# Gated convolution's input: five block groups and four plain tiles on operands without the row factor, in place of four groups and eight tiles

## The chip, the cores and the metric

The kernel runs on one core of a Trainium2 chip. The metric is the device time of one execution in microseconds (us). The kernel before was run three times, and the median counts. One further execution was recorded by the hardware profiler, and every duration in this document that is read from a trace of the kernel before comes from it.

## What is computed

The reference is a four-layer decoder trunk in float32 for one sequence of 512 positions and 1024 features: attention, a gated MLP, a gated short convolution, a gated MLP. Each layer normalises its input, computes a branch and adds it to the residual. Only the third layer's input is touched here:

```python
def rms_norm(x, g):
    xf = x.astype(jnp.float32)
    y = xf * lax.rsqrt(jnp.mean(xf * xf, axis=-1, keepdims=True) + EPS)
    return (y * g.astype(jnp.float32)).astype(x.dtype)

def causal_dwconv(x, w):
    k = w.shape[0]
    s = x.shape[1]
    xp = jnp.pad(x, ((0, 0), (k - 1, 0), (0, 0)))
    return sum(xp[:, j:j + s] * w[j] for j in range(k))

def short_conv_mixer(h, norm_g, w_in, conv_w, w_out):
    xn = rms_norm(h, norm_g)
    proj = xn @ w_in
    gate_b = proj[..., :CONV_WIDTH]
    gate_c = proj[..., CONV_WIDTH:2 * CONV_WIDTH]
    u = proj[..., 2 * CONV_WIDTH:]
    y = gate_b * causal_dwconv(gate_c * u, conv_w)
    return y @ w_out
...
        h = h + conv_ffn(h, ffn_norm[layer], ffn_w_up[layer], ffn_conv[layer], ffn_w_down[layer])
```

`rms_norm` has two factors: the gain, one number for a feature, and the row factor, one number for a position (the reciprocal root of the mean square). The row factor commutes with the matrix product, so it may be applied to the operand or to the result; gate_c * u needs its square then.

## The kernel before, in words

The residual `h` lies transposed in SBUF: features on partitions in eight tiles of 128, the 512 positions along the free dimension. Every float32 matrix product is made of three passes on two halves of each operand (a high half and the rest): high by high, low by high, high by low. ACT makes a high half by a rounding copy and VectorE the low half by a subtraction (`halves_to`, L1026 to L1029; for weights of plain tiles L315 and L316).

**Two ways to make a product.** A *plain tile* (`products`, `mm3`, L336 to L338) gives 128 output features for all 512 positions: 8 feature tiles times 3 passes, 24 matmuls of 128x512. A *block group* (class `Sevens`, matmuls in `seven`, L1078) gives four such tiles by seven products of half-sized blocks, as in Strassen's scheme: each product has 24 matmuls of 128x256, a group 168. The operands of the seven products (`up.forms`: p1, p7, p6, p2, q5, q4, p3, each as hi and lo) are sums and differences of blocks of the normalised input and are the same for all groups. The weight forms are made anew for each group out of blocks X, Y, W and Z: X and Y are loaded by SyncE's queue, a second block is added into X and into Y by a transfer on GpSimd's queue (`add_block`, L1105), and VectorE adds Y+X (L1144) and Y+W (L1199). `weights_of` splits a form into `whi_p1c`, `wlo_p1c` and so on (L1027 on ACT, L1029 on VectorE).

**The stage.** `conv_seven` (from L1368) makes the 24 output tiles of the convolution's input: eight each of b, c and u. Before, it runs eight plain tiles (u and c of tiles 0 and 1, then b of tiles 0 to 3), then four block groups: groups 1 to 3 make u and c of tiles 2 to 7, group 4 makes b of tiles 4 to 7. `want_conv` (L488) lists the plain weights in order of use. `slot(g, s)` issues product s of group g and what is due beside it; `left`, `early` and `tail` take the results to where they are used: u is multiplied by c, convolved over positions (`conv`, three taps: L443 on ACT, L446 on VectorE), then multiplied by b (`times`, L1404), and its halves (`halves_in`) are the operand of the output projection that follows.

**The norm.** While the stage before ends, squares of `h` are summed (L381 on ACT, L382 on VectorE), TensorE reduces them over partitions (L410), VectorE makes the reciprocal root by a few small steps (L422 to L434), four transposes on TensorE (L396) spread it over partitions, and ACT copies it out (L397, tile `nrow_n`, in the code `norm.row`). Plain tiles don't wait for this: their operands `hs_a` and `hs_b` hold h times gain without the row factor (L372, L373), and the row factor is multiplied into their results. The block operands of before do contain it: `prepare` makes `x_prep` = h times gain times row (L1453), eight operations on VectorE, and then the seven forms (L1459, L1027, L1029). These are `chores`, steps that are issued in small portions between matmuls of the plain tiles (`work_off`), once the row exists.

**Order.** A scheduler places each engine's instructions by its own estimates, within the dependences; `pin` keeps an instruction in program order on its engine. The wrapper `InOrder` (L66 to L74) does so for all ACT and VectorE instructions while `strict[0]` is set; these then have line 74 in the profile.

Of the kernel before, what the change touches and what calls it, by code (L numbers as in the profile page):

```python
# [17 lines left out]
F32 = mybir.dt.float32  # L18
# [4 lines left out]
ALU = mybir.AluOpType  # L23
AX = mybir.AxisListType

P = 128
S = 512
NB = S // P
D = 1024
# [28 lines left out]
def trunk(  # L58
# [146 lines left out]
    def gain_of(norm, f):  # L205
        return gains[:, norm + f:norm + f + 1]
# [5 lines left out]
    def conv_tap(j, t):  # L212
        i = 24 + j * 8 + t
        return gains[:, i:i + 1]
# [51 lines left out]
    def want(dram, k0, nk, c0, n, *more):  # L266
        wanted.append((dram, k0, nk, (c0, n) + more))
# [173 lines left out]
    def causal_conv(dst, src, tap):  # L441

        act.activation(dst, src, AF.Copy, scale=tap(2))  # L443
        for j in (1, 0):
            d = 2 - j
            dve.scalar_tensor_tensor(dst[:, d:], src[:, 0:S - d], tap(j), dst[:, d:], op0=ALU.mult, op1=ALU.add)  # L446
# [636 lines left out]
    class Sevens:  # L1083
# [139 lines left out]
                if soon:  # L1223
                    self.first_sums(g + 1)

        chores, credit, ahead = (), 0.0, False

        def rate(self, g, s):
            return 1.4 if s < 4 else 1e9

        def work_off(self, us):
            if self.norm.row is None:
                return
            self.credit = min(self.credit + us, 4.0)
            while self.credit > 0 and self.chores:
                cost = next(self.chores[0], None)
                if cost is None:
                    self.chores.pop(0)
                else:
                    self.credit -= cost  # L1240
# [127 lines left out]
    def conv_seven(norm, mp, rp):  # L1368

        def block_of(g, kh, half):  # L1370
            c0 = (4 + 2 * half) * P if g == 4 else (2 - half) * D + 2 * g * P
            return conv_w_in[0][kh * 512:(kh + 1) * 512, c0:c0 + 2 * P].rearrange("(k p) c -> p k c", p=P)

        up = Sevens("c", mp, range(1, 5), block_of)
        up.norm, up.chores, up.ahead = norm, [], True
        chores, wides, room = up.chores, up.wides, []

        def eight(dt, name):
            t = rp.tile([P, 8, S], dt, tag="head", name=name)
            return t[:, 0:4, :], t[:, 4:8, :]  # L1380
        early_t, early_b = eight(F32, "early")
        ys = []

        def place(k, n):
            if not room:
                room.append(hsp.tile([P, 12, S], F32, tag="hs_a", name="hs_a_conv"))
            return room[0][:, k:k + n, :]
        up.wides_of = lambda g: {"yg": place(8, 2), "yv": place(10, 2)}

        def conv(o, src):  # L1390
            dst = early_t[:, 2 + o, :] if o < 2 else place(o, 1)[:, 0, :]
            causal_conv(dst, src, lambda i: conv_tap(i, o))
# [12 lines left out]

        def by_tile(acc):
            return acc.rearrange("p (i t) -> p i t", t=HT)

        def left(g, acc):
            if g == 4:  # L1410
                times(4, LEFT, by_tile(acc))
            else:
                up.to_wide(g, "yg", LEFT, acc)

        def early(g, acc):
            if g == 4:
                times(6, LEFT, by_tile(acc))
            else:
                u = wides[g]["yg"][:, :, LEFT]
                dve.tensor_tensor(u, u, by_tile(acc), op=ALU.mult)  # L1420
        up.left, up.early = left, early

        def tail(p, s):
            u, c = (wides[p][n] for n in ("yg", "yv"))
            if p == 4:
                if s == 0:
                    open_ys()
                    times(6, RIGHT, c[:, :, RIGHT])
                    times(4, RIGHT, u[:, :, RIGHT])
                    halves_in(4, 2)  # L1430
                elif s == 3:
                    halves_in(6, 2)
            elif s == 0:
                if p == 2:
                    halves_in(2, 2)
            elif s == 1:
                dve.tensor_tensor(u[:, :, RIGHT], u[:, :, RIGHT], c[:, :, RIGHT], op=ALU.mult)
            elif s in (3, 4):
                conv(2 * p + s - 3, u[:, s - 3, :])
            elif s == 5 and p == 1:  # L1440
                dve.tensor_tensor(place(0, 2), early_t[:, 2:4, :], early_b[:, 0:2, :], op=ALU.mult)
                times(2, slice(0, S), early_b[:, 2:4, :])
                open_ys()
            elif s == 6 and p == 1:
                halves_in(0, 2)
        up.tail = tail

        def prepare():
            x0, x1 = mp.tile([P, 4, S], F32, tag="x0", name="x0_prep"), rp.tile([P, 4, S], F32, tag="four", name="x1_prep")
            s0, s1 = (mp.tile([P, 4, HT], F32, tag=t, name=f"{t}_prep", bufs=2) for t in "XY")  # L1450
            for x, f in ((x0, 0), (x1, 4)):
                for i in range(4):
                    dve.scalar_tensor_tensor(x[:, i, :], h[:, f + i, :], gain_of(norm.base, f + i), norm.row, op0=ALU.mult, op1=ALU.mult)  # L1453
                    yield 0.75
            a, b, c, d = x0[:, :, LEFT], x0[:, :, RIGHT], x1[:, :, LEFT], x1[:, :, RIGHT]
            for n, src, made in (("p1", a, None), ("p7", s0, (a, b, ALU.subtract)), ("p6", s0, (s0, d, ALU.add)), ("p2", c, None),
                                 ("q5", s1, (b, d, ALU.subtract)), ("q4", d, None), ("p3", s0, (c, s0, ALU.subtract))):
                if made:
                    dve.tensor_tensor(src, made[0], made[1], op=made[2])  # L1459
                    yield 1.22  # L1460
                halves_to(*up.forms[n], src)
                yield 1.22

        def input_(o, u, c):
            x, y = early_t[:, 0, :], early_t[:, 1, :]
            for t, acc in ((x, u), (y, c)):
                dve.tensor_tensor(t, acc, norm.row, op=ALU.mult)
                yield 0.69
            dve.tensor_tensor(x, x, y, op=ALU.mult)
            yield 0.69  # L1470
            conv(o, x)
            yield 1.5

        def gate(o, acc):
            dve.tensor_tensor(early_b[:, o, :], acc, norm.row, op=ALU.mult)
            yield 0.69

        accs = []
        for j in range(8):
            accs.append(bank("bbbbaabb"[j]))  # L1480
            for _ in products(accs[-1], weights(), (4, 5, 6, 7, 0, 1, 2, 3)):
                up.work_off(SHARE)
            if j in (1, 3):
                chores.append(input_(j // 2, *accs[j - 1:]))
            if j == 3:
                chores.append(prepare())
            if j >= 4:
                chores.insert(0, gate(j - 4, accs[j]))
            if j == 5:
                up.load_pair(1)  # L1490
                up.add_block(1, "Y", 1, 1)
            if j == 7:
                up.weights_of(1, "p1", "X")
                up.first_sums(1)
                up.weights_of(1, "p6", "Y")
        want_conv_out()
        for s in range(28):
            up.slot(1 + s // 7, s % 7)
            if s == 20:
                sum_far(99)  # L1500
            if s == 27:
# [290 lines left out]
```

## Time and profile before

| | |
|---|---|
| median of 3 runs | 1119.16 us (1118.87 to 1119.36) |
| the profiled execution | 1119.06 us |
| its span (first to last instruction) | 1117.3 us |
| mean granted TensorE clock | 1.0 |
| TensorE's first plain tile of the stage | 610.02 us after the span's start |
| first block group | 656.12 us |
| first matmul of the output projection | 736.29 us |

Engines in the profile: PE is TensorE's matmuls, PEld its weight loads (beside PE), DVE VectorE, ACT ScalarE, POOL GpSimd, SP SyncE. A row of a timeline gives start, duration, engine, line, operation, tiles as out<-in, their sizes and a count; in brackets the idle time before it and what ended that. A row of windows gives, after the window and its length, busy time with the count of instructions of each engine asked for, then the granted clock, the share of the DMA engines and GB/s. A row of waits gives the total, the count and the longest. A row of transfers gives its count, size and median time from issue to landing. Matmuls are pipelined, so the interval from one start to the next is what counts, not the duration of one.

### The profile page before, as it was taken

To read this page: it belongs to the slowest core of one execution; us is meant where nothing else is said; L and a number is where in the kernel's file an instruction comes from. 1 tells how busy PE (TensorE), PEld (TensorE's weight loads), DVE (VectorE), ACT (ScalarE), POOL (GpSimd) and SP (SyncE) were. 2 spreads that over 40 slices of the span, in tenths; PEclk is the share of its full clock that TensorE was granted. 3 is DMA by queue.
4 is the path that set the end of the run, shared out by engine and by line. 5 is a ranking of instruction groups with operands and counts; after the bars stand their busy time and mean duration, and the time that the engine had idled before them with its cause. 6 is when DMAs were issued, how large, how long until landed. Compare 5 with 4: busy or idle time off the path is not lost.

```text
span 1117.3 us, 19714 instructions
## 1 busy us (share of the span) xinstructions
PE 1109.9 (99%) x7803; PEld 1014.2 (91%) x7803; DVE 960.8 (86%) x1483; ACT 681.2 (61%) x1006; POOL 175.4 (16%) x199
## 2 busy tenths in 40 slices
PE   9999999999999999999999999999999999999998
PEld 7888787878899999999999899988999999998886
DVE  6798888997899787898989888867899999999886
ACT  7466677655466666666557355545666656567553
POOL 4011111111012221014400001110111221014300
PEclk9999999999999999999999999999999999999999
DMA  6668877778678887899963355696879887899951
GB/s 196 169 182 202 199 175 207 190 206 227 177 174 200 204 202 177 218 271 193 226 178 81 113 145 139 138 278 168 214 185 219 195 201 181 218 260 206 231 152 57
DMA packets 176988, 210.94 MB, mean 189 GB/s; under 512 B 7580, under 2 KB 142796, under 8 KB 176896
## 3 DMA queue, kind: packets, MB, share of 16 engines
q0 software_dynamic: 50112, 92.19, 42.7%
q1 hardware_dynamic: 126624, 117.42, 33.4%
q8 instruction: 61, 1.00, 0.3%
q14 instruction: 31, 0.25, 0.1%
q10 hardware_dynamic: 160, 0.07, 0.0%
HBM read 204.68 MB, written 44.04 MB: 223 GB/s over the span
## 4 chain that ended last, share of the span: by engine, by line
PE 96%; DVE 2%; issue 1%; ACT 1%; DVEq 0%; ACTq 0%
PE psb L1078 31%; PE psa L1078 12%; PE psb L1670 11%; PE psa L1670 8%; PE psb L336 6%; PE psb L338 5%; PE psb L337 5%; PE psb L710 2%; PE psa L338 2%; PE psa L337 2%; PE psa L336 2%; PE psa L807 2%; PE psc L782 1%; PE psb L592 1%; PE psb L593 1%; PE psb L594 1%
## 5 line engine op out<-in xcount | busy, mean ns | idle before, releaser
L1078 PE MATMUL psb<-p_hi,whi_p 128*128 128x256 f32 x480 | 135.4, 282 | 0.0
L1078 PE MATMUL psb<-p_lo,whi_p 128*128 128x256 f32 x480 | 135.2, 282 | 0.0
L1078 PE MATMUL psb<-p_hi,wlo_p 128*128 128x256 f32 x480 | 135.0, 282 | 0.0
L315 ACT ACTIVATE whi<-raw 128x1024 fp32r<-128x1024 f32 (+2 forms) x81 | 83.2, 1028 | 80.3 <-PE psb L337 27.8
L316 DVE TENSOR_TENSOR wlo<-raw,whi 128x1024 fp32r<-128x1024 f32 (+2 forms) x81 | 95.8, 1183 | 20.8 <-ACT whi L315 20.2
L1078 PEld LDWEIGHTS psb<-p_hi,whi_p 128*128 128x128 f32 x480 | 91.0, 189 | 0.0
L1078 PEld LDWEIGHTS psb<-p_lo,whi_p 128*128 128x128 f32 x480 | 90.5, 189 | 0.0
L1078 PE MATMUL psa<-p_hi,wlo_p 128*128 128x256 f32 x320 | 90.2, 282 | 0.0
L1078 PE MATMUL psa<-p_lo,whi_p 128*128 128x256 f32 x320 | 90.2, 282 | 0.0
L1078 PE MATMUL psb<-q_lo,whi_q 128*128 128x256 f32 x320 | 90.2, 282 | 0.0
L1078 PE MATMUL psb<-q_hi,whi_q 128*128 128x256 f32 x320 | 90.1, 282 | 0.0
L1078 PEld LDWEIGHTS psb<-p_hi,wlo_p 128*128 128x128 f32 x480 | 90.1, 188 | 0.0
L1078 PE MATMUL psa<-p_hi,whi_p 128*128 128x256 f32 x320 | 90.0, 281 | 0.0
L1078 PE MATMUL psb<-q_hi,wlo_q 128*128 128x256 f32 x320 | 90.0, 282 | 0.0
L336 PE MATMUL psb<-hs_a,whi 128*128 128x512 f32 x192 | 79.3, 413 | 0.0
L338 PE MATMUL psb<-hs_a,wlo 128*128 128x512 f32 x192 | 76.2, 398 | 0.0
L1670 PE MATMUL psb<-act,whi 128*128 128x256 f32 x352 | 63.3, 282 | 0.0
L1078 PEld LDWEIGHTS psa<-p_hi,whi_p 128*128 128x128 f32 x320 | 60.6, 190 | 0.1
L1078 PEld LDWEIGHTS psb<-q_hi,whi_q 128*128 128x128 f32 x320 | 60.6, 189 | 0.0
L1078 PEld LDWEIGHTS psa<-p_lo,whi_p 128*128 128x128 f32 x320 | 60.3, 189 | 0.1
L1078 PEld LDWEIGHTS psb<-q_lo,whi_q 128*128 128x128 f32 x320 | 60.4, 189 | 0.0
L1078 PEld LDWEIGHTS psa<-p_hi,wlo_p 128*128 128x128 f32 x320 | 60.1, 188 | 0.0
(551 smaller groups left out, 3596.7 us busy)
## 6 DMA issues: line engine op xcount, KB each, us to landing
t<-in_ffn_w_up POOLq DMA_DIRECT2D x24, 768.0 KB, 8.0
raw<-in_attn_w_in SPq DMA_DIRECT2D x24, 512.0 KB, 5.0
t<-in_ffn_w_up POOLq DMA_DIRECT2D x12, 1024.0 KB, 10.1
X<-in_ffn_w_up SPq DMA_DIRECT2D x20, 512.0 KB, 5.0
Y<-t SPq DMA_DIRECT2D x20, 512.0 KB, 6.6
three<-t SPq DMA_DIRECT2D x20, 512.0 KB, 5.4
W<-in_ffn_w_up SPq DMA_DIRECT2D x20, 512.0 KB, 4.0
Z<-in_ffn_w_up SPq DMA_DIRECT2D x20, 512.0 KB, 5.5
```

The costliest lines, as they stand in the source:

```text
L315: return (act.activation(hi[:, at_], raw[:, at_], AF.Copy), dve.tensor_tensor(lo[:, at_], raw[:, at_], f32(hi[:, at_]), op=ALU.subtract))
L316: dve.tensor_tensor(lo[:, at_], raw[:, at_], f32(hi[:, at_]), op=ALU.subtract))
L336: made = [pe.matmul(acc, w[0], rhs[0], start=first, stop=False), pe.matmul(acc, w[0], rhs[1], start=False, stop=False), pe.matmul(acc, w[1 ...
L337: pe.matmul(acc, w[0], rhs[1], start=False, stop=False),
L338: pe.matmul(acc, w[1], rhs[0], start=False, stop=last)]
L592: pe.matmul(acc, lhs[0], w[0], start=first, stop=False)
L593: pe.matmul(acc, lhs[0], w[1], start=False, stop=False)
L594: pe.matmul(acc, lhs[1], w[0], start=False, stop=last)
L710: pe.matmul(ss[e][:, c:c + wide], ql[rows, b * P:n], kl[rows, 0:wide], start=first and b == bs[0], stop=last and b == bs[-1])
L807: pe.matmul(out_, w, t[:, first:first + step * (NB - k - 1) + 1:step, :], start=k == 0 and i == 0, stop=k == NB - 1 and i == 1)
L1078: pe.matmul(to, w[a][:, k, c], x[b][:, k, :], start=fresh and i + k + t == 0, stop=i == 1 and k == 3 and t == 2, skip_group_check=not fresh)
L1670: pe.matmul(to, l, r, start=begin and o + t == 0, stop=end and t == 2 and o == (0 if layer else 1), skip_group_check=not fresh)
```

## The change

Groups now begin at 0: five block groups make u and c of all eight tiles and b of tiles 4 to 7, and only b of tiles 0 to 3 is left to plain tiles. The block operands no longer contain the row factor. Three of the seven forms (p1, p2, q4) are plain blocks of h times gain, and their halves exist in `hs_a` and `hs_b` already: `copied` copies them by six transfers on GpSimd's queue. The other four (p7, p6, q5, p3) are made by `RawForms` out of `x_raw` = h times gain (L1299 on ACT; sums L1308; halves as before). `eager` lets these steps run before the row exists. The row factor comes later: `row2`, its square, is multiplied into u*c of each group before the convolution; the gates of tiles 0 to 3 get it as before; tiles 4 to 7, whose b comes from group 4, get it by `times(4, ...)` and `times(6, ...)`. From the third plain tile to the first product of group 0, ACT and VectorE keep program order (`strict[0]`).

```diff
     def want_conv():
-        for part, o in ((2, 0), (1, 0), (2, 1), (1, 1)) + tuple((0, o) for o in range(4)):
-            want(conv_w_in[0], 0, 8, part * D + o * P, P)
+        for o in range(4):
+            want(conv_w_in[0], 0, 8, o * P, P)
...
         def work_off(self, us):
-            if self.norm.row is None:
+            if self.norm.row is None and not self.eager:
                 return
...
-        up = Sevens("c", mp, range(1, 5), block_of)
+        up = Sevens("c", mp, range(5), block_of)
...
+        row2 = mp.tile([P, S], F32, tag="row2", name="row2")
...
+        def both(t):
+            return t[:, None, :].to_broadcast([P, 2, S])
...
             if p == 4:
                 if s == 0:
                     open_ys()
+                    times(6, slice(0, S), both(norm.row))
                     times(6, RIGHT, c[:, :, RIGHT])
...
             elif s == 1:
                 dve.tensor_tensor(u[:, :, RIGHT], u[:, :, RIGHT], c[:, :, RIGHT], op=ALU.mult)
+                if p == 3:
+                    times(4, slice(0, S), both(norm.row))
             elif s in (3, 4):
+                if s == 3:
+                    dve.tensor_tensor(u, u, both(row2), op=ALU.mult)
                 conv(2 * p + s - 3, u[:, s - 3, :])
...
+        x0, x1 = mp.tile([P, 4, S], F32, tag="x0", name="x0_raw"), rp.tile([P, 4, S], F32, tag="four", name="x1_raw")
+        raw = RawForms(up, (x0, x1), *(early_t[:, k:k + 2, :].rearrange("p i (j t) -> p (i j) t", t=HT) for k in (0, 2)))
+
+        def copied(name, k0, side):
+            for part, to in enumerate(up.forms[name]):
+                own_, at_ = (hs_now["b"], 0) if part and k0 else (hs_now["a"], 8 if part else k0)
+                pin(nc.gpsimd.dma_start(to, own_[:, at_:at_ + 4, side]))
+
         def prepare():
-            x0, x1 = mp.tile([P, 4, S], F32, tag="x0", name="x0_prep"), rp.tile([P, 4, S], F32, tag="four", name="x1_prep")
...
-                for i in range(4):
-                    dve.scalar_tensor_tensor(x[:, i, :], h[:, f + i, :], gain_of(norm.base, f + i), norm.row, op0=ALU.mult, op1=ALU.mult)
-                    yield 0.75
...
+            for f in range(4):
+                raw.take(f)
+                yield 0.6
+            raw.make("p7")
+            yield 2.4
+            for f in range(4, ND):
+                raw.take(f)
+                yield 0.6
+            raw.make("p6")
+            yield 2.4
...
         def gate(o, acc):
-            dve.tensor_tensor(early_b[:, o, :], acc, norm.row, op=ALU.mult)
-            yield 0.69
...
+            norm.scaled(lambda: dve.tensor_tensor(early_b[:, o, :], acc, norm.row, op=ALU.mult))
+
+        up.eager = True
+        chores.append(prepare())
+        copied("p2", 4, LEFT)
+        norm.scaled(lambda: dve.tensor_tensor(row2, norm.row, norm.row, op=ALU.mult))
+        for j in range(4):
+            acc = bank("b")
+            for _ in products(acc, weights(), (4, 5, 6, 7, 0, 1, 2, 3)):
                 up.work_off(SHARE)
...
+            if j < 3:
+                gate(j, acc)
+            if j == 0:
+                up.load_pair(0)
+                copied("p1", 0, LEFT)
+                up.add_block(0, "Y", 1, 1)
+                copied("q4", 4, RIGHT)
+            if j == 2:
+                strict[0] = True
+                up.weights_of(0, "p1", "X")
+                up.first_sums(0)
+        up.weights_of(0, "p6", "Y")
         want_conv_out()
-        for s in range(28):
-            up.slot(1 + s // 7, s % 7)
-            if s == 20:
+        for s in range(35):
+            up.slot(s // 7, s % 7)
+            if s == 0:
+                gate(3, acc)
+                strict[0] = False
+                raw.make("q5")
+            if s == 2:
+                raw.make("p3")
+            if s == 27:
                 sum_far(99)
```

How this moves instructions is shown at three places. The first is TensorE's queue around the spread of the norm. Before, the transposes (L396) stand in the third plain tile, `psb_7477`, after its eleventh matmul, with its last 13 and five whole tiles behind them:

```order
L337 MATMUL psb_7477<-hs_b_7202,whi_7378 128x512
L338 MATMUL psb_7477<-hs_a_7201,wlo_7379 128x512
L396 MATMUL psc_7468<-ident,ncol_n_7428 128x128 x4
L336 MATMUL psb_7477<-hs_a_7201,whi_7378 128x512
L337 MATMUL psb_7477<-hs_a_7201,whi_7378 128x512
```

Now they stand in the last plain tile, `psb_7544`; the first group's products p1 (`psa_7573`) and p7 (`psb_7608`) follow:

```order
L396 MATMUL psc_7496<-ident,ncol_n_7450 128x128 x4
L338 MATMUL psb_7544<-hs_a_7201,wlo_7434 128x512
L336 MATMUL psb_7544<-hs_a_7201,whi_7433 128x512
L337 MATMUL psb_7544<-hs_a_7201,whi_7433 128x512
L338 MATMUL psb_7544<-hs_a_7201,wlo_7434 128x512
L336 MATMUL psb_7544<-hs_a_7201,whi_7433 128x512
L337 MATMUL psb_7544<-hs_a_7201,whi_7433 128x512
L338 MATMUL psb_7544<-hs_a_7201,wlo_7434 128x512
L1078 MATMUL psa_7573<-p_hic,whi_p1c_7534 128x256
L1078 MATMUL psa_7573<-p_loc,whi_p1c_7534 128x256
L1078 MATMUL psb_7608<-p_hic,whi_p7c_7538 128x256
L1078 MATMUL psb_7608<-p_loc,whi_p7c_7538 128x256
L1078 MATMUL psa_7573<-p_hic,wlo_p1c_7535 128x256
```

The transposes have moved from 61 plain matmuls after the stage's start to 89, of 96 in all, and the fifth block matmul needs `wlo_p1c`. VectorE's queue at that place now, from the end of the reciprocal root (`ncol_n`) on, has row2 (`row_7377`, L1482), three gates (L1477) and then, kept in program order (L74), the first weight halves:

```order
L434 SCALAR_TENSOR_TENSOR ncol_n_7450<-rb_n_7471,ry_n_7467 128x4
L1029 TENSOR_TENSOR p_loc<-early,p_hic 128x1024
L1482 TENSOR_TENSOR row_7377<-nrow_n_7495 128x512
L1477 TENSOR_TENSOR early<-psb_7382,nrow_n_7495 128x512
L1477 TENSOR_TENSOR early<-psb_7432,nrow_n_7495 128x512
L1477 TENSOR_TENSOR early<-psb_7508,nrow_n_7495 128x512
L74 TENSOR_TENSOR wlo_p1c_7535<-Xc_7423,whi_p1c_7534 128x1024
L74 TENSOR_TENSOR wlo_p7c_7539<-Yc_7424,whi_p7c_7538 128x1024
L74 TENSOR_TENSOR Yc_7424<-Yc_7424,Xc_7423 128x1024
L74 TENSOR_TENSOR wlo_p6c_7570<-Yc_7424,whi_p6c_7569 128x1024
```

The four operations ahead of `wlo_p1c` all read `nrow_n`; before, the first group's `wlo_p1c` started at 653.7 us, and the row was there at 626.2. On ACT `whi_p1c`, `whi_p7c` and `whi_p6c` follow L397 in the same pinned way. The third place is VectorE's queue where the last group begins. Before:

```order
L1029 TENSOR_TENSOR wlo_q5c_8263<-Xc_7935,whi_q5c_8262 128x1024
L446 SCALAR_TENSOR_TENSOR hs_a_conv<-hs_a_conv,gains 128x511 x2
L446 SCALAR_TENSOR_TENSOR hs_a_conv<-hs_a_conv,gains 128x510 x2
L1029 TENSOR_TENSOR wlo_q4c_8296<-Yc_7936,whi_q4c_8295 128x1024
L1029 TENSOR_TENSOR wlo_p1c_8330<-Xc_8167,whi_p1c_8329 128x1024
L1133 TENSOR_TENSOR hs_a_conv<-psb_8198,P7sc_8230 128x2x256
```

And now:

```order
L1029 TENSOR_TENSOR wlo_q5c_8356<-Xc_8028,whi_q5c_8355 128x1024
L1446 TENSOR_TENSOR hs_a_conv<-hs_a_conv,row_7377 128x1024
L1029 TENSOR_TENSOR wlo_q4c_8390<-Yc_8029,whi_q4c_8389 128x1024
L446 SCALAR_TENSOR_TENSOR hs_a_conv<-hs_a_conv,gains 128x511 x2
L446 SCALAR_TENSOR_TENSOR hs_a_conv<-hs_a_conv,gains 128x510 x2
L1404 TENSOR_TENSOR hs_a_conv<-hs_a_conv,nrow_n_7495 128x1024
L1133 TENSOR_TENSOR hs_a_conv<-psb_8291,P7sc_8323 128x2x256
L1029 TENSOR_TENSOR wlo_p1c_8424<-Xc_8260,whi_p1c_8423 128x1024
```

Three operations have come between `wlo_q5c` and `wlo_p1c` of the last group: the multiplication by row2 (L1446), the one by the row (L1404) and the L1133 that stood behind. GpSimd's queue has 202 instructions in place of 194: the six copies and the two additions of group 0.

More of the change, by code (lines that the diff above doesn't have):

```diff
@@ L1224, in slot @@
                     self.first_sums(g + 1)
-        chores, credit, ahead = (), 0.0, False
+        chores, credit, ahead, eager = (), 0.0, False, False
         def rate(self, g, s):
@@ L1390, in conv @@
         def conv(o, src):
-            dst = early_t[:, 2 + o, :] if o < 2 else place(o, 1)[:, 0, :]
-            causal_conv(dst, src, lambda i: conv_tap(i, o))
+            causal_conv(place(o, 1)[:, 0, :], src, lambda i: conv_tap(i, o))
         def halves_in(o, n):
@@ L1437, in tail @@
                 dve.tensor_tensor(u[:, :, RIGHT], u[:, :, RIGHT], c[:, :, RIGHT], op=ALU.mult)
+                if p == 3:
+                    times(4, slice(0, S), both(norm.row))
             elif s in (3, 4):
+                if s == 3:
+                    dve.tensor_tensor(u, u, both(row2), op=ALU.mult)
                 conv(2 * p + s - 3, u[:, s - 3, :])
[L1440 to L1443, printed above, removed]
+            elif s == 5 and p < 2:
+                times(2 * p, slice(0, S), early_b[:, 2 * p:2 * p + 2, :])
+                if p == 1:
+                    open_ys()
             elif s == 6 and p == 1:
```

38 lines of the change are left out of this document (1 added, 37 removed).

## The prediction

> **What bounds the kernel now.** I read the page's busy times and the chain that ended last, then TensorE's waits over the whole program, then the stage that the change touches.
>
> ```profile
> PE 1109.9 (99%) x7803; PEld 1014.2 (91%) x7803; DVE 960.8 (86%) x1483; ACT 681.2 (61%) x1006; POOL 175.4 (16%) x199
> PE 96%; DVE 2%; issue 1%; ACT 1%; DVEq 0%; ACTq 0%
> engine line waited for: us in total, times, longest us
> PE psc L858 <- DVE blank L129: 1.0, 1, 1.0
> PE psa L336 <- ACT whi L315: 0.9, 1, 0.9
> 606.00:656.10 50.10, 50.10 (x240) 41.30 (x239) 46.08 (x67) 25.08 (x31) 0.00 (x0) 1.00 0.34 101
> 656.11:676.02 19.91, 19.91 (x168) 1.00 0.69 170
> 656.12 0.28 PE L1078 MATMUL psa<-p_hic,whi_p1c 128*128 128x256 f32 x1
> 736.29 0.39 PE L336 MATMUL psa<-y,whi 128*128 128x512 f32 x1
> ```
>
> TensorE is busy for 99% of the span and is 96% of the chain; its two longest waits are 1.0 and 0.9 us. So a matmul taken away is worth its whole interval, and a wait put in front of TensorE costs its whole length. The two windows hold the stage: the first all plain tiles, the second exactly one block group (168 matmuls, 19.91 us, 0.1185 each), at a granted clock of 1.00. From the first block matmul (656.12) to the first of the output projection (736.29) four groups take 80.17 us, 0.53 more than four times 19.91: that is all that the block part waits today.
>
> **What the change removes and adds on TensorE.** Four plain tiles (96 matmuls of 128x512) go, one group (168 of 128x256) comes.
>
> ```profile
> 633.80 0.39 PE L336 MATMUL psa<-hs_a,whi 128*128 128x512 f32 x1
> 644.97 0.39 PE L336 MATMUL psb<-hs_a,whi 128*128 128x512 f32 x1
> ```
>
> These rows are 48 plain matmuls apart: 11.17 us, 0.2327 each. The gain is 96 x 0.2327 = 22.34, the price 168 x 0.1185 = 19.91: **-2.43 us**. No wait may come with it if that is to arrive.
>
> **The row factor at the start of the first group.** Before, the four transposes that spread the norm (L396) come after 61 plain matmuls, and 131 more run before the first group. After, they come after 89 of 96, so 7 plain matmuls are left, then four block matmuls on the high weight halves, and then one that needs wlo_p1c. On VectorE wlo_p1c now stands behind row2 and three gates, and all four need the row.
>
> ```profile
> 624.95 0.61 PE L396 MATMUL psc<-ident,ncol_n 128*128 128x128 f32 x4
> 625.32 0.48 PE L336 MATMUL psb<-hs_a,whi 128*128 128x512 f32 x1
> 625.60 0.60 ACT L397 ACTIVATE nrow_n<-psc 128x512 f32<-128x512 f32 x1 [2.20 <-PE psc L396]
> 626.23 1.29 DVE L1467 TENSOR_TENSOR early<-psb,nrow_n 128x512 f32<-128x512 f32 x2 [1.37 <-ACT nrow_n L397]
> 711.36 1.23 DVE L1029 TENSOR_TENSOR wlo_p1c<-Xc,whi_p1c 128x1024 fp32r<-128x1024 f32 x1 [0.56 <-ACT whi_p1c L1027]
> 712.50 0.68 DVE L1133 TENSOR_TENSOR hs_a_conv<-psb,P7sc 128x512 f32<-128x512 f32 x1
> 713.10 1.22 DVE L1029 TENSOR_TENSOR wlo_p7c<-Yc,whi_p7c 128x1024 fp32r<-128x1024 f32 x1
> ```
>
> I count from the first transpose. VectorE's first use of the row starts 626.23 - 624.95 = 1.28 later. A 128x512 operation holds VectorE 0.60 (712.50 to 713.10), a 128x1024 one 1.14 (711.36 to 712.50) and is complete after 1.23. So wlo_p1c starts at 1.28 + 4 x 0.60 = 3.68 and is there at 4.91. TensorE resumes at 0.37 (625.32), spends 7 x 0.2327 + 4 x 0.1185 = 2.10, and stands at 2.47. It waits **+2.44 us**. That is as long as the gain. ACT's whi_p1c and whi_p7c, pinned behind nrow, are ready inside the same pause. Afterwards wlo_p7c, Yc+Xc and wlo_p6c follow at 1.14 each while p1 and p7 give 2.8 us each, so the pause doesn't repeat. It would fall below 2.44 only if TensorE reached the transposes late for another reason; that reason costs its own time.
>
> **The convolution chain in front of the last group.** u\*row2 (L1446, 128x1024) joins each group's chain, and near the last group norm.row on tiles 4 and 5 (L1404, 128x1024) comes ahead of wlo_p1c, with an L1133 that stood behind it. What stands there now:
>
> ```profile
> 697.13 1.28 POOL L1105 DMA_DIRECT2D Xc<-in_conv_w_in  x1 [18.95 <-ACT psb L1185]
> 704.70 1.06 ACT L1027 ACTIVATE whi_q5c<-Xc 128x1024 fp32r<-128x1024 f32 x1 [4.00 <-DMA Xc<-in_conv_w_in]
> 705.80 1.23 DVE L1029 TENSOR_TENSOR wlo_q5c<-Xc,whi_q5c 128x1024 fp32r<-128x1024 f32 x1 [2.61 <-ACT whi_q5c L1027]
> 706.94 2.73 DVE L446 SCALAR_TENSOR_TENSOR hs_a_conv<-hs_a_conv,gains 128x511 f32<-128x511 f32 x4
> 709.58 1.22 DVE L1029 TENSOR_TENSOR wlo_q4c<-Yc,whi_q4c 128x1024 fp32r<-128x1024 f32 x1
> 709.78 0.60 ACT L1129 ACTIVATE hs_a_conv<-psa 128x512 f32<-128x512 f32 x1 [1.36 <-DVE hs_a_conv L446]
> 710.28 1.05 ACT L1027 ACTIVATE whi_p1c<-Xc 128x1024 fp32r<-128x1024 f32 x1
> 713.58 0.28 PE L1078 MATMUL psa<-p_hic,whi_p1c 128*128 128x256 f32 x1
> ```
>
> The Xc addition issued by POOL at 697.13 releases whi_q5c 7.57 us later. VectorE has idled 2.61 by then, and its queue from 705.80 sets when wlo_p1c is done: 711.36 + 1.23 = 712.59. Its first use is the third matmul, 713.58 + 2 x 0.1185 = 713.82: 1.23 to spare. After the change stand from 705.80: wlo_q5c 1.14, u\*row2 1.14, wlo_q4c 1.14, L446 2.64, L1404 1.14, L1133 0.60; wlo_p1c starts at 713.60 and is done at 714.83. TensorE waits **+1.0 us**, if the addition lands as late as today.
>
> ```profile
> Xc<-in_conv_w_in POOLq DMA_DIRECT2D x4, 512.0 KB, 6.9
> Yc<-in_conv_w_in POOLq DMA_DIRECT2D x3, 512.0 KB, 9.7
> DMA to landing us min/median/max: 5.7/6.4/7.5
> ```
>
> The last row counts all eight loads of Xc, the first only POOL's. Landing in 6.4 instead of 7.57 would take the whole wait away; landing in Yc's 9.7 would add 2.1 to it. I take 1.0, since the row at 697.13 is the same transfer at the same place. The Trainium skill speaks against that size: "DMA: Bandwidth & Descriptors", section "Anatomy of one DMA — SWDGE (gpsimd) path", fits 2.0 us plus bytes/436e3 for a GpSimd transfer, which for 512 KB is an estimate of 3.2 us, and by it this wait would be nil and the sum 0.0. The trace disagrees: no load of Xc landed in under 5.7.
>
> **What I cost at nothing.** *The six copies* (128x4x256 each, POOL queue): the trace of before has no such copy. The first group's p1 operands come from hs_a.
>
> ```profile
> 615.14 0.72 ACT L372 ACTIVATE hs_a<-h,gains 128x512 fp32r<-128x512 f32 x1 [1.84 <-DVE h L1606]
> 617.43 0.74 DVE L373 SCALAR_TENSOR_TENSOR hs_a<-h,gains,hs_a 128x512 fp32r<-128x512 f32 x1
> 618.09 0.68 DVE L382 TENSOR_TENSOR nacc_n<-nacc_n,sq_n 128x512 f32<-128x512 f32 x1
> 619.40 0.95 PE L410 MATMUL psc<-ones,nacc_n 128*128 128x1 f32 x8
> t<-t POOLq DMA_DIRECT2D x1, 1024.0 KB, 5.5
> 736.19 1.23 DVE L1029 TENSOR_TENSOR y_lo<-hs_a_conv,y_hi 128x1024 fp32r<-128x1024 f32 x1
> L337 PE MATMUL psa<-y_lo,whi x4: 391/396/400, 739.3 to 745.6; 128*128 128x512 f32 x4
> L1453 DVE SCALAR_TENSOR_TENSOR x_prep<-h,gains,nrow_n 128x512 f32<-128x512 f32 x8 | 6.0, 746 | 0.0
> ```
>
> hs_a is complete at 618.2, and the first group begins when four plain tiles are done, where the fifth began today (633.80). That leaves 15.6 us for two copies, and as much for the Yc addition queued behind them, which whi_p7c needs. The nearest rows are 5.5 (1 MB between buffers) to 9.7. Two more places in the queue at 2.8 each (9.7 - 6.9, the two neighbours' difference) give 9.7 + 5.6 = 15.3: just covered. If the three ran one after another at 7.5 each, 22.5, they would be 6.9 late. I take 0 and keep that end in a small chance. *Four x_raw operations* on ACT stand ahead of the last two hs_a: ACT idles 1.84 before 615.14 and four at 0.61 (two neighbours of L372's shape) fill 2.4, so hs_a is up to 0.6 later; the sums at 619.40 have 0.63 of slack behind 618.09 + 0.68. *L1404 at the end of the stage* makes the second y_lo 1.14 later; it ends at 737.4 today (736.19 start) and its first use is at 739.3. *The forms* leave VectorE (eight x_prep at 0.75) and stand on ACT (61% busy): no one waits for them now.
>
> **Sum.** -2.43 + 2.44 + 1.0 = +1.0 us. The profiled execution took 1119.06 (span 1117.3 and 1.76 around it), 0.10 under the median, so the changed kernel takes **1120.1 us**.
>
> **Rivals.**
> *Only the start waits* (0.17): Xc lands in about 6.4, the last group doesn't wait: -2.43 + 2.44, **1119.1**. For it: the median of eight loads. Against it: the same transfer took 7.57.
> *The gain arrives* (0.13): wlo_p1c is not held by the row, because gates and row2 overlap what I count in series, and Xc is early: 1119.06 - 2.43 = **1116.6**, or 1116.1 if today's 0.53 goes too. Against it: wlo_p1c is behind them on one in-order engine, and 2.44 is a sum of measured intervals.
> *Slower* (0.25): the queue of POOL, with eight more transfers, lands the Xc addition of the fourth group later than now. Place: wlo_q5c, and behind it the chain above. Each microsecond beyond 7.57 is one of TensorE's waits; beyond 9.0 the kernel is slower than the bound below, and at 9.7 it is **1122.2**. The late copies of the first group (+6.9, **1127.0**) are in this chance with 0.04. So is a lower clock: the Trainium skill ("TensorE: Matmul & The Clock Gate", Part 1) halves TensorE's clock after an idle window of about 3.4 us. No row here shows a pause above 1.0 or a clock below 1.00, and my pause of 2.44 is shorter; with a half clock for one product of 24 (2.84 us by 24 x 0.1185) the price would be 2.8, **1122.9**, and I give it 0.02 of the 0.25.
>
> **How the numbers follow.** Forecast 0.45, only the start 0.17, gain 0.13, slower 0.25. A measurement tells about 0.2% from no change, 2.2 us: 1116.9 to 1121.4 is "same". Forecast and first rival lie inside it, so same is 0.62, faster 0.13, slower 0.25. The range goes from 1117.0, which leaves the full gain out, to 1122.8, which takes in the late landing of 9.7 and leaves out late copies and the clock.
>
> **What would show it.** The profile after should have L396 seven plain matmuls ahead of the first L1078, TensorE's longest wait there (about 2.4, released by VectorE's wlo_p1c at L74), and a second one of about 1 at the last group's p1. A first group without that wait proves the second step wrong; a fourth q5 that waits for the Xc transfer is the slower case; p_hi or p_lo of p1 released by a transfer is the late copies.

## The result, and the profile after

The changed kernel takes 1122.74 us (median of 6 runs, 1121.79 to 1123.68) against 1118.72 (6 runs) for the kernel before: ratio 1.0035, 95% interval 1.0022 to 1.0048. It is slower, by 2.5 to 5.4 us, and the loss is clear of noise. The forecast was 1120.1.

The profiled execution took 1121.85 us, with a span of 1119.7. The page, and TensorE's longest waits (columns as before):

```profile
PE 1109.1 (99%) x7875; PEld 1016.9 (91%) x7875; DVE 964.0 (86%) x1482; ACT 687.7 (61%) x1018; POOL 182.4 (16%) x207
PE 90%; DVE 4%; issue 3%; DMA 2%; ACT 1%; SPq 0%; DVEq 0%; ACTq 0%; POOLq 0%
...
PE psa L336 <- ACT whi L315: 1.3, 1, 1.3
PE psa L1078 <- DVE wlo_p1c L74: 1.3, 1, 1.3
PE psc L858 <- DVE blank L129: 1.0, 1, 1.0
PE psb L1078 <- DVE hs_a_conv L1133: 0.9, 1, 0.9
```

TensorE's busy time fell by only 0.8 us for 2.4 us of fewer matmuls, and its share of the chain from 96% to 90%. Two waits are new in this list: wlo_p1c at line 74 and L1133. The stage of either kernel in one window, from the first plain matmul to the first matmul of the output projection, before:

```profile
610.02:736.29 126.27, 126.27 (x879) 117.02 (x877) 111.35 (x135) 65.33 (x79) 11.75 (x11) 1.00 0.58 143
```

and after (TensorE alone):

```profile
609.12:738.64 129.52, 126.45 (x951) 0.99 0.73 171
```

The stage is **3.25 us longer**, with a granted clock of 0.99. What stands behind it is as long as before (381.06 and 381.01 us to the end of the span); the stage began 0.90 earlier, but that start lies between 608.6 and 610.1 in all but one of the profiles here, so it isn't put down to the change. So what the profile shows of the loss lies in this stage. TensorE's timeline of the changed kernel at the first group:

```profile
630.79 0.60 PE L396 MATMUL psc<-ident,ncol_n 128*128 128x128 f32 x4
...
632.63 0.40 PE L338 MATMUL psb<-hs_a,wlo 128*128 128x512 f32 x1
633.02 0.39 PE L1078 MATMUL psa<-p_hic,whi_p1c 128*128 128x256 f32 x1
633.25 0.28 PE L1078 MATMUL psa<-p_loc,whi_p1c 128*128 128x256 f32 x1
633.97 0.38 PE L1078 MATMUL psb<-p_hic,whi_p7c 128*128 128x256 f32 x1 [0.44 <-DVE early L1477]
634.19 0.28 PE L1078 MATMUL psb<-p_loc,whi_p7c 128*128 128x256 f32 x1
635.73 0.49 PE L1078 MATMUL psa<-p_hic,wlo_p1c 128*128 128x256 f32 x1 [1.26 <-DVE wlo_p1c L74]
636.02 0.41 PE L1078 MATMUL psa<-p_hic,whi_p1c 128*128 128x256 f32 x1
```

The seven plain matmuls behind the transposes take 1.88 us in place of 1.63, the two p1 matmuls 0.94 in place of 0.24, the two p7 1.76 in place of 0.24: a pause of 0.25 + 0.70 + 1.52 = **2.47 us**. The row at 633.97 names a gate, but ACT's whi_p7c, behind its copy of the row and whi_p1c, ends only at 633.92, and p7 waits the same 0.44 with two gates gone (below): the first part of the pause is ACT's two high halves, and its end is set by wlo_p1c. VectorE in that time does what the order said:

```profile
632.05 0.69 DVE L1482 TENSOR_TENSOR row<-nrow_n 128x512 f32<-128x512 f32 x1 [1.28 <-ACT nrow_n L397]
632.67 1.88 DVE L1477 TENSOR_TENSOR early<-psb,nrow_n 128x512 f32<-128x512 f32 x3
634.46 1.22 DVE L74 TENSOR_TENSOR wlo_p1c<-Xc,whi_p1c 128x1024 fp32r<-128x1024 f32 x1
```

And then something that no row of before showed. Windows over the same place (length, busy time of each engine, granted clock, DMA share, GB/s):

```profile
633.00:635.70 2.70, 1.03 (x5) 0.59 (x4) 2.70 (x5) 0.91 (x1) 0.00 (x0) 1.00 0.01 2
635.70:637.00 1.30, 1.27 (x6) 1.27 (x7) 1.27 (x2) 0.00 (x0) 0.00 (x0) 0.56 0.00 0
637.00:638.00 1.00, 1.00 (x7) 1.00 (x6) 1.00 (x1) 0.00 (x0) 0.00 (x0) 0.50 0.00 0
638.00:639.00 1.00, 1.00 (x6) 1.00 (x6) 0.07 (x1) 0.82 (x1) 0.37 (x1) 0.50 0.00 0
639.00:640.00 1.00, 1.00 (x9) 1.00 (x9) 0.73 (x1) 0.24 (x1) 1.00 (x2) 0.87 0.00 0
640.00:645.00 5.00, 5.00 (x45) 5.00 (x44) 2.89 (x4) 2.73 (x4) 1.26 (x1) 1.00 1.00 153
```

When TensorE resumes its clock is at half speed, for some 3.4 us. The remaining 22 matmuls of p1 take 4.23 us, 0.192 each, in place of 2.61: **1.62 us** more. The third place is the last group, first the engines ahead of its p1:

```profile
698.52 1.28 POOL L1105 DMA_DIRECT2D Xc<-in_conv_w_in  x1 [19.63 <-ACT psb L1185]
704.47 1.06 ACT L1027 ACTIVATE whi_q5c<-Xc 128x1024 fp32r<-128x1024 f32 x1 [3.06 <-DMA Xc<-in_conv_w_in]
705.56 1.23 DVE L1029 TENSOR_TENSOR wlo_q5c<-Xc,whi_q5c 128x1024 fp32r<-128x1024 f32 x1 [1.23 <-ACT whi_q5c L1027]
...
711.74 1.23 DVE L1404 TENSOR_TENSOR hs_a_conv<-hs_a_conv,nrow_n 128x1024 f32<-128x1024 f32 x1
711.82 0.60 ACT L1129 ACTIVATE hs_a_conv<-psa 128x512 f32<-128x512 f32 x1 [2.53 <-DVE hs_a_conv L446]
712.31 1.05 ACT L1027 ACTIVATE whi_p1c<-Xc 128x1024 fp32r<-128x1024 f32 x1
713.48 1.22 DVE L1029 TENSOR_TENSOR wlo_p1c<-Xc,whi_p1c 128x1024 fp32r<-128x1024 f32 x1
```

p1 of the last group starts at 713.93 and takes 3.52 in place of 2.84: **0.68 us**. Then its p3:

```profile
733.74 1.23 DVE L1404 TENSOR_TENSOR hs_a_conv<-hs_a_conv,nrow_n 128x1024 f32<-128x1024 f32 x1
734.88 0.69 DVE L1133 TENSOR_TENSOR hs_a_conv<-psb,P7sc 128x512 f32<-128x512 f32 x1
735.72 0.36 PE L1078 MATMUL psb<-p_hic,whi_p3c 128*128 128x256 f32 x1 [0.94 <-DVE hs_a_conv L1133]
```

p3 adds into the bank (of PSUM, where TensorE's sums lie) that L1133 still has to read, and L1133 stands behind the multiplication of tiles 6 and 7 by the row. The product before p3 takes 3.92 to p3's start in place of 2.84: **1.08 us**. Together -2.43 + 2.47 + 1.62 + 0.68 + 1.08 = +3.42, 0.17 more than the 3.25 measured; before, three other products took 0.1 to 0.3 us over their 2.84, and those small waits are mostly gone.

### The profile page after: what moved, and what is told of

Read it like the earlier page. It is cut to its first block, busy times and chain, and to the rows that moved or that the text cites. A ratio compares the mean times of both kernels' runs of the same rounds, so it can differ in the third digit from the quotient of the medians.

```text
span 1119.7 us, 19897 instructions
## 1 busy us (share of the span) xinstructions
PE 1109.1 (99%) x7875; PEld 1016.9 (91%) x7875; DVE 964.0 (86%) x1482; ACT 687.7 (61%) x1018; POOL 182.4 (16%) x207
## 4 chain that ended last, share of the span: by engine, by line
PE 90%; DVE 4%; issue 3%; DMA 2%; ACT 1%; SPq 0%; DVEq 0%; ACTq 0%; POOLq 0%
PE psb L1078 28%; PE psa L1078 12%; PE psb L1679 11%; PE psa L1679 8%; PE psb L336 5%; PE psb L338 5%; PE psb L337 5%; PE psb L710 2%; PE psa L807 2%; PE psa L338 1%; PE psa L336 1%; PE psa L337 1%; DMA Xc<-in_conv_w_in 1%; PE psc L782 1%; PE psb L592 1%
## 5 line engine op out<-in xcount | busy, mean ns | idle before, releaser
L315 ACT ACTIVATE whi<-raw 128x1024 fp32r<-128x1024 f32 (+2 forms) x77 | 79.0, 1027 | 72.2 <-PE psb L337 22.2
L316 DVE TENSOR_TENSOR wlo<-raw,whi 128x1024 fp32r<-128x1024 f32 (+2 forms) x77 | 90.9, 1181 | 23.7 <-ACT whi L315 23.2
L336 PE MATMUL psb<-hs_a,whi 128*128 128x512 f32 x176 | 72.7, 415 | 0.0
L338 PE MATMUL psb<-hs_a,wlo 128*128 128x512 f32 x176 | 70.1, 398 | 0.0
```

The costliest lines, as they stand in the source:

```text
L315: return (act.activation(hi[:, at_], raw[:, at_], AF.Copy), dve.tensor_tensor(lo[:, at_], raw[:, at_], f32(hi[:, at_]), op=ALU.subtract))
L316: dve.tensor_tensor(lo[:, at_], raw[:, at_], f32(hi[:, at_]), op=ALU.subtract))
L336: made = [pe.matmul(acc, w[0], rhs[0], start=first, stop=False), pe.matmul(acc, w[0], rhs[1], start=False, stop=False), pe.matmul(acc, w[1 ...
L338: pe.matmul(acc, w[1], rhs[0], start=False, stop=last)]
```

## The experiments

All but one alter the changed kernel. Times wander by several us between runs of one kernel (1120.16 to 1126.65 in eleven of the changed one), so beside the ratio to the kernel before stands the length of the stage in the profiled execution (before 126.27, changed 129.52).

**The clock by itself.** The pause is filled, not shortened:

```diff
...
+                    if dummies and i + k == 0:
+                        if t == 1:
+                            other = bank("c")
+                            for d in range(dummies):
+                                nxt = pe.matmul(other[:, 0:HT], w[0][:, 0, c], x[0][:, 0, :], start=d == 0, stop=d == dummies - 1)
+                                behind(nxt, m)
+                                m = nxt
+                            dull[0] = m
+                        if t == 2:
+                            behind(m, dull[0])
...
```

> The changed kernel with sixteen more 128x256 matmuls (operands p_hi and whi_p1c, into a psc bank that nobody reads) put behind the first two matmuls of group 0's p1. They fill TensorE's wait for wlo_p1c (2.5 us in the changed kernel) and don't shorten it. Theory A, the clock: the granted clock of 0.50 at 636 to 639 us follows from the pause, so with TensorE busy it stays at 1.00, p1 of group 0 runs at 0.119 per matmul in place of 0.192, and the kernel gains 1.6 us: 1121.1 against 1122.7. Rival: the low clock has another cause (the change of shape, the copies' traffic); then it stays, and the time is within 0.4 us of 1122.7.

Measured: 1120.42 us, ratio 1.0015 (1.0006 to 1.0024); the stage is 127.46.

```profile
633.98:636.69 2.71, 2.64 (x22) 1.00 0.01 2
636.69:639.38 2.69, 2.69 (x22) 1.00 0.00 0
```

The first window is the time of the pause, now full of matmuls, and the second is the 22 matmuls of p1: 2.69 us at clock 1.00 in place of 4.23. The pause is as long as it was (2.71 us from the first p1 matmul to the first one that needs wlo_p1c, in either kernel), so the low clock follows from TensorE's idleness in it. Of the 2.06 us that the stage is shorter, 1.54 are these 22 matmuls; 0.27 lie in q5 and q4 of the last group, which the edit doesn't touch. Only 1 of the 11 runs had a mean clock under 0.999. A second run put in six matmuls in place of sixteen:

> The changed kernel with six more matmuls in the pause in place of sixteen (their results are read by nobody). If TensorE's share of work in the whole pause decides the clock, six of sixteen leave it low or partly low; if an unbroken idle stretch does, the stretch is now some 1.3 us and the clock stays at 1.00, as it did behind an unbroken 1.7 us in the run with the gates behind.

A single execution: the unbroken idle time was 1.25 us (ended by wlo_p1c), the clock 1.00 throughout, the stage 128.03. Whether six are enough isn't shown by it, because the unaltered kernel also keeps a mean clock of 1.0 in some executions (3 of 11, below).

**The row chain.** First, row2 and two gates behind the first weight halves:

```diff
...
-        norm.scaled(lambda: dve.tensor_tensor(row2, norm.row, norm.row, op=ALU.mult))
...
-            if j < 3:
-                gate(j, acc)
+            accs.append(acc)
+            if j == 0:
+                gate(0, acc)
...
+        gate(1, accs[1])
         up.weights_of(0, "p6", "Y")
+        norm.scaled(lambda: dve.tensor_tensor(row2, norm.row, norm.row, op=ALU.mult))
+        gate(2, accs[2])
```

> The changed kernel with row2 and two of the three gates issued behind the first weight halves of group 0 in place of ahead of them; one gate and nrow stay ahead. Theory A (the row chain sets wlo_p1c): three times 0.60 leave the chain, whi_p1c on ACT ends last now, so the pause at the first group falls from 2.5 to about 1.1 us, and with so short a pause the clock stays at 1.00: 1.4 + 1.6 = 3.0 us less, about 1119.7. If the clock still falls, only 1.4 less: 1121.3. Rival (the copies or the loads of group 0 set the start): no change, 1122.7.

Measured: 1122.28, ratio 1.0032 (1.0018 to 1.0047). A miss: 3 us were expected, and the change in time can't be told from none. The profile shows why: the pause did shrink, from 2.47 to about 1.15 us (what is left is ACT's whi_p1c and whi_p7c, for which p7 waits 0.44), and the clock there stayed at 1.00, but the scheduler put the first matmul of q5 behind only two of p2, and it waited:

```profile
636.20:637.48 1.28, 0.84 (x5) 1.00 0.00 0
637.48:640.17 2.69, 2.69 (x24) 1.00 0.00 0
645.64:650.51 4.87, 3.23 (x27) 1.00 1.10 242
...
647.67 0.39 PE L1078 MATMUL psb<-q_hic,whi_q5c 128*128 128x256 f32 x1 [1.64 <-ACT Xsc L1139]
```

In the profiled execution 1.8 us went back there: ACT's copy Xsc stands behind whi_q5c, which waited until 646.08 for POOL's addition into X. The stage was 128.19, 1.3 shorter; the times show less of that than they should, and two of the nine runs were above 1125. The profiled one had a low clock at 50 to 70 us, far ahead of the stage (0.90 and 0.93 in windows of 10 us, 1.7 us of time), and its stage began at 612.26 in place of 609.12. What the other runs lost stays open. A second try keeps these moves and takes the row out of the way altogether: the first weight halves are made behind the first plain tile, and ACT's copy of the row and all gates stand behind them:

```diff
...
-            acc = bank("b")
+            acc = bank("abbb"[j])
...
+            if j == 0:
+                up.weights_of(0, "p1", "X")
+                norm.first.append(up.made[0, "p1"])
             if j == 2:
                 strict[0] = True
-                up.weights_of(0, "p1", "X")
                 up.first_sums(0)
...
             act.activation(self.row, t, AF.Copy)
+            if self.first:
+                behind(made, self.first[0][0])
```

> The changed kernel with wlo_p1c and whi_p1c made after the first plain tile, ahead of the row, and with row2 and the gates behind; the first plain tile takes a psa bank, so that p7 doesn't wait for a gate. Theory A: no wait at the first group (2.5 less) and no low clock (1.6 less): 4.1 us less, about 1118.6, which leaves the two waits near the last group. Rival: behind the row chain the operand copies or the Yc addition are the next wait; then p7 or p1 of group 0 wait for a transfer, and the gain is under 3 us.

Measured: 1118.83, ratio 0.9999 (0.9990 to 1.0008); 4 us less than the changed kernel's ratio, as expected. Stage 125.95. The next waits at the first group are small: q5 again (0.59 us) and p6 (0.44).

```profile
632.17 0.60 PE L398 MATMUL psc<-ident,ncol_n 128*128 128x128 f32 x4
...
633.07 0.28 PE L1083 MATMUL psa<-p_hic,whi_p1c 128*128 128x256 f32 x1
633.18 0.28 PE L1083 MATMUL psa<-p_loc,whi_p1c 128*128 128x256 f32 x1
633.30 0.28 PE L1083 MATMUL psa<-p_hic,wlo_p1c 128*128 128x256 f32 x1
```

The transposes are even later here, and p1 runs straight behind the last plain matmul: their place doesn't matter once the halves don't wait for the row.

**The last group.** The two multiplications by the row are held back:

```diff
-                    times(6, slice(0, S), both(norm.row))
+                    behind(times(6, slice(0, S), both(norm.row)), up.joined[4])
...
-                    times(4, slice(0, S), both(norm.row))
+                    behind(times(4, slice(0, S), both(norm.row)), up.made[4, "p7"][1])
```

> The changed kernel with the two multiplications by norm.row (tiles 4 and 5, tiles 6 and 7) held behind wlo_p7c of the last group and behind the last group's second L1133. Theory: the 0.7 us that the last group's p1 waits and the 1.1 us that its p3 waits (p3 may not overwrite its bank before L1133 has read it, and L1133 stands behind a 1.14 us multiplication) go: 1.8 us less, about 1120.9. Rival: L1446 and the late Xc addition set these waits, or the multiplications only move the wait to the output projection; then less than 0.6 us is gained.

Measured: 1120.66, ratio 1.0013 (1.0004 to 1.0022), about 2.4 us less than the changed kernel; stage 128.02. The wait at p3 is gone:

```profile
733.05 0.68 DVE L1134 TENSOR_TENSOR hs_a_conv<-psb,P7sc 128x512 f32<-128x512 f32 x1
733.66 1.21 DVE L316 TENSOR_TENSOR wlo<-raw,whi 128x1024 fp32r<-128x1024 f32 x1
734.79 0.68 DVE L1134 TENSOR_TENSOR hs_a_conv<-psb,Xsc 128x512 f32<-128x512 f32 x1
735.39 1.21 DVE L1405 TENSOR_TENSOR hs_a_conv<-hs_a_conv,nrow_n 128x1024 f32<-128x1024 f32 x1
```

At p1 0.22 us of 0.68 are left, and 0.40 come back at the output projection, where y_lo is late. The profile thus accounts for 1.1 (stage 1.5 less 0.4), and its low clock at the first group was there as in the changed kernel. The rest stays open: the mean clock was 1.0 in 4 of these 11 runs and in none of the changed kernel's first six, but in 3 of its next eleven.

**The copies.** The three forms are computed, not copied:

```diff
+            raw.make("p1")
+            yield 1.2
             raw.make("p6")
...
-        copied("p2", 4, LEFT)
...
-                copied("p1", 0, LEFT)
...
-                copied("q4", 4, RIGHT)
...
+                raw.make("p2")
                 raw.make("q5")
             if s == 2:
+                raw.make("q4")
```

> The changed kernel with p1, p2 and q4 made by ACT and VectorE out of x_raw in place of the six copies. Theory (the copies cost nothing, and what hurts is VectorE's queue at the row): the three forms add 3 x 1.14 us ahead of the row in VectorE's queue, the transposes come some 2 us later, and the pause grows from 2.5 to about 4.5 us, now with a low clock in nearly every run: 2 us slower than the changed kernel, 1.005. Rival (the copies' traffic or their landing is part of the loss): it is as fast as the changed kernel or faster.

Measured: 1128.17, ratio 1.0077 (1.0064 to 1.0090), by the ratios 4.8 us slower than the changed kernel beside it, where 2 were expected. So copying is the cheaper way. The run puts other work in the copies' place and doesn't show by itself that they cost nothing; that rests on the profile of the changed kernel, in which no engine of the first group waits for them.

```profile
636.63 0.36 PE L1078 MATMUL psb<-p_hic,whi_p7c 128*128 128x256 f32 x1 [2.45 <-DVE early L1479]
638.86 0.58 PE L1078 MATMUL psa<-p_hic,wlo_p1c 128*128 128x256 f32 x1 [1.77 <-DVE wlo_p1c L74]
```

**The changed kernel again, and versions.** The changed kernel ran once more beside the others:

> The changed kernel itself, unaltered, beside the three others on one chip. 1.0035 times the kernel before, as in its first runs, if these six runs were typical; nearer 1.002 if the low clock behind the pause comes only in part of the executions (the altered kernel that kept the pause had a mean clock of 1.0 in 4 of 11 runs and 0.998 or 0.999 in the others).

1122.88, ratio 1.0034 (1.0024 to 1.0044), stage 129.48: the same, and in the profiled execution the low clock again (0.57 from 636.0 to 639.6). It wasn't there in every execution: the mean clock was 0.997 or 0.998 in 8 of the 11 and 1.0 in 3 (1120.16, 1120.9 and 1122.88 us). Both alterations together:

> The changed kernel with both alterations that gained alone: first weight halves ahead of the row, and the two multiplications by norm.row behind the joins of the last group. Theory: the two are at different places and add up. The first alone gave 0.9999 times the kernel before, the second took 2 us off the changed kernel; 0.9999 less 1.8 us gives 0.998, about 2 us under the kernel before, which is the 2.4 us of fewer matmuls less 0.5 of small waits. Rival: what the second saves is only given back at the output projection (its profile showed y_lo waited for); then 0.999 or more.

1118.33, ratio 0.9992 (0.9983 to 1.0000); stage 125.92, with 0.99 us at the last group's p1. The gain on the changed kernel is 4.7 us by the ratios, 1.6 less than the two alone gave in sum, so the 0.998 that was expected didn't come. With the first gate behind too:

> As the run before, and the first gate behind wlo_p7c and the sum Y+X of group 0, so that the addition into X is issued 0.6 us earlier. Theory: with the pause at group 0 gone the next wait there is q5 of group 0 (0.6 us in the profile of the first alteration), which waits for that addition; 0.5 us less than the run before, 0.9975. Rival: the landing varies by more than that; no difference from the run before.

1117.77, ratio 0.9987 (0.9979 to 0.9996), stage 124.73: faster than the kernel before by 0.4 to 2.3 us, and the lowest median here. The 0.5 us less than the run before can't be told from none by the intervals, and q5 of the first group still waits 0.33 us. The last run went after what was left at the last group: whi_p1c is issued ahead of L1129, and the row of tiles 6 and 7 goes behind the first L1133.

> The version with an early first addition into X, and two more moves near the last group: whi_p1c of a group ahead of ACT's copy L1129 (which waits for the whole convolution chain of VectorE), and the multiplication of tiles 6 and 7 by norm.row right behind the first of the two L1133 in place of the second. Theory: the wait at the last group's p1 that is left after the norm.row multiplication was moved (0.2 to 1.0 us in four profiles) is whi_p1c on ACT, behind L1129, and goes; the 0.4 us for y_lo at the output projection go too: 0.9 us less than 0.9987 times the kernel before, 0.998. Rival: wlo_p1c on VectorE, behind u times row2 and the four L446, is late without it too; then the wait stays over 0.3 us and the time is 0.9985 or more.

```profile
706.47 1.04 ACT L1031 ACTIVATE whi_p1c<-Xc 128x1024 fp32r<-128x1024 f32 x1
709.08 0.60 ACT L1134 ACTIVATE hs_a_conv<-psa 128x512 f32<-128x512 f32 x1 [1.57 <-DVE hs_a_conv L450]
709.58 1.05 ACT L1031 ACTIVATE whi_p7c<-Yc 128x1024 fp32r<-128x1024 f32 x1
```

1118.16, ratio 0.9998 (0.9989 to 1.0007): no gain. The wait at p1 is gone, so it was ACT's whi_p1c behind the convolution chain; but 0.64 us come up at the next p2 and 1.00 at the output projection, where y_lo is later, not earlier. The stage with that projection's wait is 126.36, against 125.12 (124.73 + 0.39) for the version before it.

## Why the prediction was right, and where it fell short

- *Fewer matmuls, -2.43:* right. With the waits mostly removed, the version with the early halves and the late row comes to a stage 1.5 us shorter than before, 1.1 with the wait that follows; what is missing to 2.43 are the waits that its profile still shows.
- *The row factor at the first group, +2.44:* right, 2.47 measured, in the chain of the order: row, row2, three gates, wlo_p1c. Here the rows give the forecast's own steps: wlo_p1c starts 3.67 us after the first transpose (forecast 3.68). Taking row2 and two gates out of this chain halved the pause, and taking the row out of it ended it.
- *The clock:* the step that failed most. It stood among the rivals with 0.02 and a price of 2.8, because the pause was thought too short and no row of before had a pause above 1.0 us. It came in the profiled execution and cost 1.62 us there. The mean clock fits one such fall in all six first runs (0.996 or 0.998; 3.4 us at half speed take 0.0015 off the mean) and in 8 of the 11 later ones, but only the two profiled executions show where it lay, and the kernel before had 0.998 in 6 of its 75 executions beside the experiments. The Trainium skill ("TensorE: Matmul & The Clock Gate", Part 1) has the mechanism and the halving, and the trace agrees with 0.50; it names an idle window of about 3.4 us, and here 2.9 us with four matmuls in them (632.86, where the first p1 matmul was due, to 635.73) did it. The price was over-sized because the clock came back within p1.
- *The last group's p1, +1.0:* right in place, 0.68 in size, with luck in it. VectorE's queue was summed rightly: from wlo_q5c's start to wlo_p1c's end it takes 9.14 us, 9.03 in the forecast. But the addition into Xc, on which the term was made to hang, released whi_q5c 5.95 us after its issue and not 7.57, by which the forecast would have had no wait; it was issued 15.4 us ahead of that p1 in place of 16.45, which took most of this back. And the reason was half the story: VectorE's queue (713.48) and ACT's whi_p1c, behind L1129 (713.36), end together, and moving L1404 alone left 0.2 to 1.0 us.
- *The end of the stage, nothing:* wrong. "L1404 at the end of the stage makes the second y_lo 1.14 later" looked only at who reads its result. The wait was one step beside it: L1133, queued behind L1404 on VectorE, releases the bank that p3 adds into. 1.08 us.
- *The copies, nothing:* right as far as the profile goes. No row shows TensorE, ACT or VectorE waiting for them in the changed kernel, and the run that makes the forms instead is slower. They landed in 5.3 to 13.2 us:

```profile
p_hic<-hs_a POOLq DMA_DIRECT2D x2, 512.0 KB, 5.9
p_loc<-hs_b POOLq DMA_DIRECT2D x1, 512.0 KB, 5.3
p_loc<-hs_a POOLq DMA_DIRECT2D x1, 512.0 KB, 8.9
q_hic<-hs_a POOLq DMA_DIRECT2D x1, 512.0 KB, 12.5
q_loc<-hs_b POOLq DMA_DIRECT2D x1, 512.0 KB, 13.2
```

- *The sum:* the forecast of +1.0 lacks 1.62 (clock) and 1.08 (p3) and has 0.32 too much (p1): +3.4, against 3.25 in the stage. The measured median lies at the upper end of the range and beyond the bound for "same", so the case named slower was the true one; its mechanism, a late Xc addition in the fourth group, was not. That the range held is luck: its upper end was set for that late addition and was meant to leave the clock out, and the wait at p3 was in no case at all. Between the medians are 4.0 us, with an interval that holds 3.25; whether more than the stage's 3.25 was lost stays open.

## What to carry to other kernels

When an operation goes off an operand and onto results, look for what stands behind it in its engine's queue: here four short multiplications stood ahead of the one split that TensorE needed. Ordering three of them behind it halved the pause, and making the split before the row existed ended it. A product that adds into a bank waits for the bank's last reader, so every operation put ahead of that reader counts, also where its own result has time. On an engine whose longest wait was 1.0 us, price a new pause of a few microseconds with the slower clock behind it as well, by the granted clock of a trial.

## What the runs showed of the hardware that was not expected

The low clock (0.50) lasted some 3.4 us behind the pause of 2.9 us with four matmuls in it, in three profiled executions (the changed kernel twice, the run with the two multiplications held back). In the run with the forms computed, where TensorE waited 2.45 and 1.77 us one behind the other, it lasted twice as long (0.51 over the 7.0 us from 637.2), and the 22 matmuls of p1 took 4.86 us. An unbroken idle time of 1.64 us (the run with the gates behind) and of 1.25 (the run with six matmuls in the pause) left it at 1.00, in one execution each.

No edge follows from this. In the run with the gates behind, the clock also fell to half from 58.0 us on, for 3.4 us, and from its first instruction up to there TensorE hadn't been idle for more than 0.6 us at a stretch. Between 50 and 58 us it was busy for 7.45 us there, as in the changed kernel's profile, whose clock stayed at 1.00. And the changed kernel itself kept a mean clock of 1.0 in 3 of its 17 executions. So the length of one idle stretch doesn't decide it in these runs, and the same pause doesn't bring the fall every time.
